# Banded attention stage: the rotary half-swap transfers are put out behind a pair's second transpose, and weight loads are asked for twelve units sooner

## The chip, the cores and the metric

The kernel runs on one core of one Trainium2 chip. The metric is the device time of one execution in microseconds; the time of a kernel is the median of its runs. Three runs of the kernel before took 1186.71, 1188.02 and 1188.46 us, so its time is 1188.02 us. Durations and waits in this text come from one further execution, taken under the hardware profiler: it took 1186.6 us, and its span from the first to the last instruction was 1184.9 us.

The engines are PE (matrix products; PEld is its weight load), DVE (vector), ACT (scalar functions), POOL (GpSimd) and SP, which here does nothing but issue DMA transfers. Each engine takes its instructions strictly in the order in which they stand in the program and waits in place where an input is missing.

## The reference

One decoder layer on 2048 tokens of width 1024. A normalised, modulated input `h` is multiplied by one wide matrix, and the product is cut into the inputs of two attentions. The second, the banded one, is what the change touches: queries and keys are rotated by position, each block of 128 queries sees its own and the preceding block of keys, and a learned sink joins the softmax.

```python
proj = h @ w_in[l]
qa, ka, va, fa, za, qb, kb, vb, zb = jnp.split(proj, split_points, axis=-1)
oa = forgetting_attention(qa, ka, va, fa + b_fgate[l])      # causal, 8 heads
oa = oa * jax.nn.silu(za)
qb = rope(qb, positions); kb = rope(kb, positions)
ob = sliding_window_sink_attention(qb, kb, vb, sinks[l])    # window 128, 8 query heads, 2 kv heads
ob = ob * jax.nn.silu(zb)
y = jnp.concatenate([oa, ob], axis=-1) @ w_out[l]
x = x + gate[:, None, :] * rms_norm(y, g_post[l])

def rope(x, positions):            # x1, x2: the two halves of a head's 64 columns
    return concatenate([x1 * cos - x2 * sin, x2 * cos + x1 * sin])
```

## The kernel before

Every matrix operand is split into a high and a low fp16 part, and a product is made of three fp16 products. The input projection is cut into **groups** of eight **units** (`proj_units`, L328; `value_units`, L346): one group makes 512 tokens of 128 output columns in one PSUM bank, of which there are three. The groups stand in one list, `punits`, and `fill` issues them unit by unit. A **key** such as `qb2`, `zb3` or `va1` names 128 columns of the weight matrix. What its weights need before their first unit hangs on `events`, at a lead counted in units: the load (`w_load`, 46 units ahead), the largest absolute value (`w_max`, L223, 36), the exchange of that value (`w_back`, 26), the scale, the high part (`w_high`, L266, on ACT) and the two halves of the low part (`w_low`, L272, on DVE). The raw weights have two buffers.

Work that follows a group, its evacuation, is put off by `after(n, f)`: `f` is issued at the n-th following `tick`.

**The banded stage** (about 160 to 414 us of the profile) runs 32 windows, `Pair(j, i)`: two query blocks of two heads each. It walks through the windows with four ticks to a window, and fills about 8.5 units of the projection between the ticks. In step n the program issues, in this order: the maxima of window n on DVE (L865), after the second tick the output products of window n-2 on PE (`pv`, L914), after the third tick the four exponentials of window n on ACT (L876), one tick later the rounding of its probabilities to fp16 on ACT (L893) with a DMA transpose of that high part (L894), one tick later, at the first tick of step n+1, the subtraction that leaves the low part on DVE (L898) with a second DMA transpose (L899), and at the end of step n the score products of window n+1 on PE (L851). The fp32 scores of a window have one buffer, so the maxima of window n+1 cannot start before the low part of window n is done. `pv` of a window needs both of its transposes.

**The rotation of a query group** is done in `evac_rope`. One tick after the group ACT copies the product to `qf` (L716), and SP issues four transfers of 32 partitions each that swap the halves into `qs` (L718). One tick later DVE multiplies the product by the cosine into `qc` (L721). In the banded stage (`turn_lag` 1) POOL multiplies `qs` by the sine at tick 6 (L731), DVE adds the two at tick 7 (L732), ACT rounds the sum to the high part of `stb` at tick 8 (L733), and DVE makes the low part at tick 9 (L725). `qf` and `qs` have one buffer each. The scores of the windows of that query group read `stb`.

**Weight loads in this stage** are not issued where they are asked for. `w_load` puts them on the list `queued`, and `load_now` empties it on SP right behind the second transpose of a window (or when the largest value is needed and the load is still on the list). Loads asked for before the stage are issued by POOL at once. The four swap transfers, in contrast, go to SP at the copy's tick, wherever that falls between the transposes.

After the stage come the causal attention (455 to about 1000 us) and the output projection. The change does not touch their instructions.

Of the kernel before, what the change touches and what calls it, by code (L numbers as in the profile page):

```python
# [14 lines left out]
AF = mybir.ActivationFunctionType  # L15
ALU = mybir.AluOpType
# [24 lines left out]
def hybrid_layer(  # L41
# [17 lines left out]
    V, A, G, PE, SP = nc.vector, nc.scalar, nc.gpsimd, nc.tensor, nc.sync  # L59
# [74 lines left out]
    sinT = swc.tile([P, S], F32, name="sinT")  # L134
# [26 lines left out]
    def kappa(pw, name):  # L161
        kap = const.tile([P, 1], F32, name=f"kap_{name}")
        V.tensor_scalar(kap[:], pw[:], pH[:], 0.125, op0=ALU.mult, op1=ALU.mult)
        return kap
# [22 lines left out]
    def after(n, f):  # L187
        late.append([n, f])
# [9 lines left out]
    kaps_seen = []  # L198
    first = ("kb", "vb", "zb0", "zb1")

    queued, banded = [], [False]

    def load_now():
        todo, queued[:] = queued[:], []
        for key, pieces in todo:
            w_load(key, pieces, SP)

    def w_load(key, pieces, eng=None):
        if banded[0] and eng is None:
            queued.append((key, pieces))  # L210
            return
        width = VB if key == "vb" else P
        raw = (vbw if key == "vb" else wpool).tile([P, KT, width], F32, tag="wraw", name=f"wr_{key}")
        o = 0
        for col0, n in pieces:
            (eng or G).dma_start(raw[:, :, o:o + n], w_in0[:, col0:col0 + n].rearrange("(k p) n -> p k n", p=P))
            o += n
        wq[key] = [raw]

    def w_max(key):  # L220
        if any(h[0] == key for h in queued):
            load_now()
        V.tensor_reduce(wmx[:, 0:1], wq[key][0][:], axis=AX.XY, op=ALU.max, apply_absolute_value=True)  # L223
        md, mt = mx_d[len(kaps_seen) % 3], wmt[len(kaps_seen) % 2]
        V.transpose(mt[:], wmx[:])
        kaps_seen.append(key)

        def put():
            G.dma_start(md[:].rearrange("(b j) o -> b (j o)", b=4),
                    mt[:].rearrange("(b r) j -> b r j", b=4)[:, 0, :])  # L230
            wq[key].append(md)

        if lag[0]:
            after(lag[0], put)
        else:
            put()

    def w_back(key):
        mxr = mxp.tile([P, P], F32, tag="mxr", name="mxr")
        G.dma_start(mxr[:], wq[key].pop().rearrange("p o -> (p o)").partition_broadcast(P))  # L240
        wq[key].append(mxr)

    def w_scale(key):

        floor = key[:2] == "qk"
        raw, mxr = wq[key]
        if key in first:
            mx2 = mxr
        else:
            mx2 = sm(1, "w_mx2")  # L250
            V.tensor_reduce(mx2[:], mxr[:], axis=AX.X, op=ALU.max)
        pw = sm(1, "w_pw")
        pow2_floor(pw[:], mx2[:], "w_p2")
        if floor:
            V.tensor_tensor(pw[:], pw[:], pfl[:], op=ALU.max)
        sw = sm(1, "w_sw")
        V.reciprocal(sw[:], pw[:])
        V.tensor_scalar(sw[:], sw[:], 2.0 ** 14, None, op0=ALU.mult)
        wq[key] = [raw, pw, sw]

    def w_high(key):
        raw, pw, sw = wq[key]
        width = VB if key == "vb" else P
        pool = vbw if key == "vb" else wpq if key[0] in "qk" else wpool
        whl = pool.tile([P, 2, KT, width], F16, tag="whl", name=f"wh_{key}")
        A.activation(whl[:, 0], raw[:], AF.Identity, scale=sw[:])  # L266
        wq[key].append(whl)

    def w_low(key, part, parts=2):
        raw, pw, sw, whl = wq[key]  # L270
        ks = slice(KT * part // parts, KT * (part + 1) // parts)
        V.scalar_tensor_tensor(whl[:, 1, ks], raw[:, ks], sw[:], whl[:, 0, ks], op0=ALU.mult, op1=ALU.subtract)  # L272
        if part == parts - 1:
            wq[key] = whl
            pws[key] = pw
# [9 lines left out]
    def col(name):  # L285
        return const.tile([P, 1], F32, name=name)

    def w_done(key):

        kind, j = key[:2], key[2:]  # L290
        pw = pws[key]
        if kind == "qk":
            kap = kappa(pw, key)
            scl[key] = col(f"scl_{key}")
            V.tensor_scalar(scl[key][:], kap[:], kap[:], 0.125, op0=ALU.mult, op1=ALU.mult)
            isc[key] = col(f"isc_{key}")
            V.reciprocal(isc[key][:], scl[key][:])
        elif kind == "qb":
            kap = kappa(pw, key)
            scl[key] = col(f"scl_{key}")  # L300
            V.tensor_scalar(scl[key][:], kap[:], kaps["kb"][:], 0.125, op0=ALU.mult, op1=ALU.mult)
        elif kind == "va":
            kaps[key] = kappa(pw, key)
        else:
            czs[key] = col(f"cz_{key}")
            V.tensor_scalar(czs[key][:], pw[:], pH[:], 2.0 ** -29, op0=ALU.mult, op1=ALU.mult)
            n = int(j) + (4 if kind == "zb" else 0)
            V.tensor_tensor(fac8[:, n:n + 1], kaps["vb" if kind == "zb" else f"va{j}"][:], czs[key][:], op=ALU.mult)

    def pieces(key):  # L310
        kind, j = key[:2], int(key[2:] or 0)
        if kind == "vb":
            return [(OFF_VB, P), (OFF_FA, 8)]
        if kind == "qk":
            return [(OFF_QA + j * 64, 64), (OFF_KA + j * 64, 64)]
        return [({"qb": OFF_QB, "kb": OFF_KB, "va": OFF_VA, "za": OFF_ZA, "zb": OFF_ZB}[kind] + j * P, P)]
# [133 lines left out]
    with tc.manual_schedule():  # L450
# [89 lines left out]
        rest, parts = TWO_PI, []  # L540
# [163 lines left out]
    turn_lag = [0]  # L704

    def evac_rope(ci, finish, pool):
        cols_ = slice(ci * CH, (ci + 1) * CH)

        def evac(ps, free):
            qf = swt.tile([P, CH], F32, tag="qf", name="qf")  # L710
            qs = swt.tile([P, CH], F32, tag="qs", name="qs")
            qc = op_.tile([P, CH], F32, tag="tz", name="qc")
            stg = (pool or abp).tile([P, 2, CH], F16, tag="st", name="stb")

            def copy():
                A.activation(qf[:], ps, AF.Copy, scale=PS_SCALE)  # L716
                for r in range(4):
                    SP.dma_start(qs[32 * r:32 * r + 32, :], qf[32 * (r ^ 1):32 * (r ^ 1) + 32, :])  # L718

            def cos():  # L720
                V.scalar_tensor_tensor(qc[:], ps, PS_SCALE, cosT[:, cols_], op0=ALU.mult, op1=ALU.mult)  # L721
                free()

            def low():
                V.tensor_tensor(stg[:, 1, :], qc[:], stg[:, 0, :], op=ALU.subtract)  # L725
                finish(stg)

            after(1, copy)
            after(2, cos)
            d = turn_lag[0]  # L730
            after(5 + d, lambda: G.tensor_tensor(qs[:], qs[:], sinT[:, cols_], op=ALU.mult))  # L731
            after(6 + d, lambda: V.tensor_tensor(qc[:], qc[:], qs[:], op=ALU.add))  # L732
            after(7 + d, lambda: A.activation(stg[:, 0, :], qc[:], AF.Copy))  # L733
            after(8 + d, low)

        return evac

# [188 lines left out]

    pkeys, punits = [], []

    def add(key, us):
        if key not in pkeys and key not in ("kb", "vb"):
            at = len(punits) - (24 if key[:2] == "za" else 0)
            leads = (46, 36, 26, 15, 11, 8, 7, 5) if key[:2] in ("va", "zb") else (46, 36, 26, 14, 9, 6, 4, 3)
            fs = (lambda: w_load(key, pieces(key)), lambda: w_max(key), lambda: w_back(key), lambda: w_scale(key),
                  lambda: w_high(key), lambda: w_low(key, 0), lambda: w_low(key, 1), lambda: w_done(key))
            for n, f in enumerate(fs):
                if key == "zb0":
                    if n >= 3:
                        events.setdefault(n + 9, []).append(f)  # L940
                elif key == "zb1":
                    if n >= 3:
                        events.setdefault((18, 20, 22, 24, 25)[n - 3], []).append(f)
                else:
                    events.setdefault(max(at - leads[n], n), []).append(f)
        if key not in pkeys:
            pkeys.append(key)
        punits.extend(us)
# [3 lines left out]
    for kind, j in (("zb", 0), ("zb", 1), ("va", 0), ("zb", 2), ("zb", 3), ("va", 1), ("va", 2)):  # L952
        key = f"{kind}{j}"
# [55 lines left out]
    N_PRO = len(punits)  # L1009
# [74 lines left out]
    with swa_order:  # L1084
# [18 lines left out]
        for n, wd in enumerate(windows):  # L1103
            goal = base + (N_SWA - base) * (n + 1) // NW
            todo = goal - pos[0]
# [27 lines left out]
        tick()  # L1133
        banded[0] = False
        load_now()
    swa.close()
    swx.close()
# [382 lines left out]
    with tc.manual_schedule():  # L1520
# [28 lines left out]
        for s, stp_ in enumerate(steps):  # L1549
# [7 lines left out]
            todo = []  # L1557
# [97 lines left out]
```

## Time and profile before

| | |
|---|---|
| median of 3 runs | 1188.02 us (1186.71 to 1188.46) |
| profiled execution | 1186.6 us, span 1184.9 us |
| PE busy over the span | 1122.8 us, 95% |
| DVE, ACT, POOL busy | 919.1, 677.6, 165.9 us |
| PE idle from 155 to 414 us | 259.0 us of time, 244.85 us busy |

The last row adds five stretches of the table of windows (155 to 200, 200 to 250, 250 to 300, 300 to 350, 350 to 414 us; PE busy 43.54, 47.10, 47.21, 46.88 and 60.12 us).

How to read what follows. A row of the timeline has the start in us, the duration, the engine, the line, the operation with output and input, how many instructions are merged in it, and in brackets how long the engine sat idle before it and what ended that. Rows of SP show the time that the issue of a transfer took on its queue, not when the data landed. A row of the table of windows has the stretch, its length, PE's busy time and count, the clock that was granted to PE as a share of full speed, the busy share of the DMA engines and GB/s.

### The profile page before, as it was taken

Reading aid. Unit: us, or ns where it says so; the run is one execution under the profiler, and the core shown is the slowest. Engines: PE = TensorE matmul, PEld = TensorE weight load, DVE = VectorE, ACT = ScalarE, POOL = GpSimd, SP = SyncE. Lnnn points to the kernel's source line nnn. Section 1 sums busy time; section 2 is a strip of 40 time slices with the busy share of each in tenths; the row PEclk is TensorE's granted clock in tenths of the full one; section 3 lists DMA queues with packets and bytes.
Section 4 is the critical chain, followed back from the end, with each engine's and each line's share of the span. In section 5 each row is a group of like instructions: output and inputs, shape, how many; then the busy total and the mean of one; then the engine's idle time right before and its main releaser. Section 6 shows DMA issues by size and latency. Waiting matters only on the chain. (4 is left out here: it accounts for less than half of the span.)

```text
span 1184.9 us, 27012 instructions
## 1 busy us (share of the span) xinstructions
PE 1122.8 (95%) x10490; PEld 655.1 (55%) x10490; DVE 919.1 (78%) x2329; ACT 677.6 (57%) x1122; POOL 165.9 (14%) x302
## 2 busy tenths in 40 slices
PE   5899998999989999999999999999999979999996
PEld 1466556644459855555555555555555545555553
DVE  6776577888787657889888897888878897767665
ACT  4676445565456434666766666666766788333331
POOL 1001122233232201211111111011000100000000
PEclk9999999999999999999999999999999989999999
DMA  9645336587667722333323323133121154465652
GB/s 331 213 137 158 94 88 123 113 150 143 141 132 119 130 63 70 78 93 78 85 68 103 75 61 86 45 90 64 40 48 46 59 156 156 147 191 168 210 172 78
DMA packets 162452, 136.36 MB, mean 115 GB/s; under 512 B 95356, under 2 KB 139428, under 8 KB 162324
## 3 DMA queue, kind: packets, MB, share of 16 engines
q1 hardware_dynamic: 152532, 106.65, 35.8%
q0 software_dynamic: 9456, 27.72, 8.9%
q8 instruction: 82, 1.34, 0.5%
q14 instruction: 46, 0.38, 0.1%
q10 hardware_dynamic: 336, 0.26, 0.1%
HBM read 70.97 MB, written 25.18 MB: 81 GB/s over the span
## 5 line engine op out<-in xcount | busy, mean ns | idle before, releaser
L1312 ACT ACTIVATE p<-sta,lift,scl_qk 128x1024 f32<-128x1024 f32 (+2 forms) x160 | 171.7, 1073 | 99.2 <-PE sta L1308 90.7
L328 PE MATMUL bk<-hT,wh_qk 128*128 128x512 f16 x768 | 194.6, 378 | 0.0
L1458 PE MATMUL bk<-wohl,oz 128*128 128x512 f16 x768 | 172.4, 379 | 1.9 <-ACT wohl L1398 0.8
L1323 DVE TENSOR_TENSOR pha<-p,pha 128x1024 f16<-128x1024 f32 (+2 forms) x160 | 169.3, 1058 | 0.2 <-ACT pha L1320 0.2
L1320 ACT ACTIVATE pha<-p 128x1024 f16<-128x1024 f32 (+2 forms) x160 | 148.1, 926 | 35.0 <-POOL p L1316 29.6
L1261 DVE TENSOR_REDUCE a_m<-bk 128x1 f32<-128x512 f32 x192 | 129.8, 684 | 43.6 <-PE bk L1258 43.1
L1458 PEld LDWEIGHTS <-oz 128*128 128x128 f16 x768 | 74.4, 99 | 83.9 <-issue 1.8
L1307 PE MATMUL sta<-T 128*128 128x512 f16 (+1 forms) x320 | 110.7, 351 | 10.5 <-ACT p L1312 10.5
L1333 PE MATMUL poa<-vt,pha 128*128 128x65 f16 x1088 | 117.6, 194 | 2.3 <-DVE ona L1342 2.3
L1336 PE MATMUL poa<-vt,pha 128*128 128x65 f16 x1088 | 117.2, 193 | 1.4 <-DVE pha L1323 1.4
L1335 PE MATMUL poa<-vt,pha 128*128 128x64 f16 x1088 | 117.5, 195 | 0.0
L328 PEld LDWEIGHTS <-wh_qk 128*128 128x128 f16 x768 | 72.4, 97 | 74.7 <-issue 0.6
L1333 PEld LDWEIGHTS <-pha 128*128 128x128 f16 x1088 | 102.4, 97 | 16.8 <-DVE ona L1342 3.2
L1258 PE MATMUL bk<-T 66*128 66x512 f16 (+2 forms) x320 | 109.9, 350 | 1.0 <-DVE a_m L1261 1.0
L1308 PE MATMUL sta<-T 69*128 69x512 f16 (+1 forms) x320 | 109.3, 352 | 0.0
L1335 PEld LDWEIGHTS <-pha 128*128 128x128 f16 x1088 | 101.7, 98 | 13.6 <-issue 0.3
L1336 PEld LDWEIGHTS <-pha 128*128 128x128 f16 x1088 | 101.5, 99 | 1.6 <-DVE pha L1323 1.6
L328 PE MATMUL bk<-hT,wh_za 128*128 128x512 f16 x384 | 99.8, 378 | 0.0
L346 PE MATMUL bk<-wh_va,hT 128*128 128x128 f16 x1536 | 94.3, 221 | 1.7 <-DVE wh_va L272 1.7
L328 PE MATMUL bk<-hT,wh_zb 128*128 128x512 f16 x384 | 92.7, 384 | 2.2 <-DVE wh_zb L272 2.2
L346 PEld LDWEIGHTS <-hT 128*128 128x128 f16 x1536 | 89.0, 99 | 8.3 <-issue 5.9
L1316 POOL TENSOR_SCALAR_AFFINE_SELECT p<-p 128x256 f32<-128x256 f32 x64 | 33.0, 515 | 420.6 <-ACT p L1312 417.9
(487 smaller groups left out, 1860.5 us busy)
## 6 DMA issues: line engine op xcount, KB each, us to landing
wa<-in_w_ada_dram SPq DMA_DIRECT2D x16, 512.0 KB
z_d<-tz POOLq DMA_DIRECT2D x32, 256.0 KB, 3.0
T<-stq SPq DMA_DIRECT2D x128, 64.0 KB
T<-o_d SPq DMA_DIRECT2D x16, 512.0 KB
T<-z_d SPq DMA_DIRECT2D x16, 512.0 KB
xr<-in_x_dram SPq DMA_DIRECT2D x16, 512.0 KB
out_dram<-yg SPq DMA_DIRECT2D x15, 512.0 KB
xt<-in_x_dram SPq DMA_DIRECT2D x12, 512.0 KB
```

Source lines behind the costliest of these rows:

```text
L328: PE.matmul(ps, whl[:, a, k, :], hT[ci][:, b, k, :], start=(k == 0 and n == 0), stop=(k == KT - 1 and n == 2))
L346: PE.matmul(ps[:, u * P:(u + 1) * P], hT[ci][:, a, k, u * P:(u + 1) * P], whl[:, b, k, :], start=(k == 0 and n == 0), stop=(k == KT - 1 an ...
L1258: PE.matmul(mx[:, :w], T[0:XM, 0, i * P:(i + 1) * P], T[0:XM, 2, pc * CH:pc * CH + w], start=True, stop=True)
L1261: V.tensor_reduce(m3[:, u, pc:pc + 1], mx[:, :w], axis=AX.X, op=ALU.max)
L1307: PE.matmul(self.st[:, o:o + w], T[:, 3, kb_], T[:, 1, qc], start=True, stop=False)
L1312: A.activation(self.p32[:, :self.w], self.st[:, :self.w], AF.Exp, scale=scl[f"qk{self.hd}"][:], bias=lift[:])
L1320: A.activation(self.ph[:, 0, :self.w], self.p32[:, :self.w], AF.Copy)
L1323: V.tensor_tensor(self.ph[:, 1, :self.w], self.p32[:, :self.w], self.ph[:, 0, :self.w], op=ALU.subtract)
L1333: PE.matmul(po[:, u, :], ph[:, 0, pq], vt[:, b, hd, 0:65], start=(self.first and n == 0 and u == 0), stop=False)
L1335: PE.matmul(po[:, u, 0:64], ph[:, 0, pq], vt[:, b, hd, 65:VW], start=False, stop=False)
L1336: PE.matmul(po[:, u, :], ph[:, 1, pq], vt[:, b, hd, 0:65], start=False, stop=(self.last and n == len(self.blocks) - 1))
L1458: PE.matmul(py, self.hl[:, i, k, :], w_slot(8 * j + k)[:, cc], start=(k == 0 and m_ == 0), stop=(k == KT - 1 and m_ == 2))
```

## The change

In the banded stage the copy no longer issues the swap. It puts it, with the four later steps of the rotation, on a list `swaps`; `load_now` empties that list ahead of the weight loads, so the swap goes out behind a window's second transpose, and the sine multiply, the add, the high part and the low part follow 4, 5, 6 and 7 ticks after that. Outside the stage everything is as before. And the loads of all keys that are asked for from the stage's first units on, `qk0` and the `qb`, `zb` and `va` keys, have a lead of 58 units in place of 46.

```diff
     def load_now():
+        todo, swaps[:] = swaps[:], []
+        for f in todo:
+            f()
         todo, queued[:] = queued[:], []
         for key, pieces in todo:
             w_load(key, pieces, SP)
...
             def copy():
                 A.activation(qf[:], ps, AF.Copy, scale=PS_SCALE)
+                if banded[0]:
+                    swaps.append(lambda: (swap(), rest(4)))
+                else:
+                    swap()
+                    rest(4 + turn_lag[0])
+
+            def swap():
                 for r in range(4):
                     SP.dma_start(qs[32 * r:32 * r + 32, :], qf[32 * (r ^ 1):32 * (r ^ 1) + 32, :])
+
+            def rest(d):
+                after(d, lambda: G.tensor_tensor(qs[:], qs[:], sinT[:, cols_], op=ALU.mult))
+                after(d + 1, lambda: V.tensor_tensor(qc[:], qc[:], qs[:], op=ALU.add))
+                after(d + 2, lambda: A.activation(stg[:, 0, :], qc[:], AF.Copy))
+                after(d + 3, low)
...
             after(1, copy)
             after(2, cos)
-            d = turn_lag[0]
-            after(5 + d, lambda: G.tensor_tensor(qs[:], qs[:], sinT[:, cols_], op=ALU.mult))
-            after(6 + d, lambda: V.tensor_tensor(qc[:], qc[:], qs[:], op=ALU.add))
-            after(7 + d, lambda: A.activation(stg[:, 0, :], qc[:], AF.Copy))
-            after(8 + d, low)
...
-    pkeys, punits = [], []
+    pkeys, punits, N_PRO = [], [], 10 ** 6
...
+            if at > N_PRO and (key == "qk0" or key[:2] not in ("qk", "za")):
+                leads = (58,) + leads[1:]
```

The order on PE is the same, instruction for instruction. On SP, here the issues from the first transpose of window 4 to the second of window 7, before (`ptb` is what a transpose writes, `sp` the rounded probabilities, `qs` and `qf` the swap, `wr` raw weights):

```order
L894 DMA_TRANSPOSE ptb<-sp_1938 128x8x128
L718 DMA qs<-qf 32x512 x4
L899 DMA_TRANSPOSE ptb<-sp_1936 128x8x128
L894 DMA_TRANSPOSE ptb<-sp_1937 128x8x128
L899 DMA_TRANSPOSE ptb<-sp_1938 128x8x128
L216 DMA wr_qb_2733<-in_w_in_dram 128x8x128
L894 DMA_TRANSPOSE ptb<-sp_1936 128x8x128
L718 DMA qs<-qf 32x512 x4
L899 DMA_TRANSPOSE ptb<-sp_1937 128x8x128
L894 DMA_TRANSPOSE ptb<-sp_1938 128x8x128
L899 DMA_TRANSPOSE ptb<-sp_1936 128x8x128
```

and the same windows with the change:

```order
L905 DMA_TRANSPOSE ptb<-sp_1938 128x8x128
L910 DMA_TRANSPOSE ptb<-sp_1936 128x8x128
L728 DMA qs<-qf 32x512 x4
L219 DMA wr_qb_2580<-in_w_in_dram 128x8x128
L905 DMA_TRANSPOSE ptb<-sp_1937 128x8x128
L910 DMA_TRANSPOSE ptb<-sp_1938 128x8x128
L905 DMA_TRANSPOSE ptb<-sp_1936 128x8x128
L910 DMA_TRANSPOSE ptb<-sp_1937 128x8x128
L728 DMA qs<-qf 32x512 x4
L905 DMA_TRANSPOSE ptb<-sp_1938 128x8x128
L910 DMA_TRANSPOSE ptb<-sp_1936 128x8x128
```

No swap stands between the two transposes of a window any more (before, this was so in windows 4, 6, 14, 21 and 23), and the load of `qb2` stands one window sooner. The other loads that SP issues in the stage move by one window too, `zb2` and `va1` by two.

On DVE, from the low part of window 9 to that of window 10 (the rows of the maxima, L865 or L876, are thinned to the last), before:

```order
L732 TENSOR_TENSOR qc<-qc,qs 128x512
L898 TENSOR_TENSOR sp_1937<-sm__3131,sp_1936 128x1024
...
L868 TENSOR_SCALAR b_nb<-b_m 128x2
L725 TENSOR_TENSOR stb<-qc,stb 128x512
L920 TENSOR_TENSOR on<-pob,b_ri 128x256
L272 SCALAR_TENSOR_TENSOR wh_qb_3255<-wr_qb_2733,w_sw,wh_qb_3255 128x512
L721 SCALAR_TENSOR_TENSOR qc<-bk_135,cosT 128x512
L272 SCALAR_TENSOR_TENSOR wh_qb_3255<-wr_qb_2733,w_sw,wh_qb_3255 128x512
L898 TENSOR_TENSOR sp_1936<-sm__3237,sp_1938 128x1024
```

and with the change:

```order
L909 TENSOR_TENSOR sp_1937<-sm__3131,sp_1936 128x1024
...
L879 TENSOR_SCALAR b_nb<-b_m 128x2
L732 TENSOR_TENSOR qc<-qc,qs 128x512
L931 TENSOR_TENSOR on<-pob,b_ri 128x256
L275 SCALAR_TENSOR_TENSOR wh_qb_3256<-wr_qb_2580,w_sw,wh_qb_3256 128x512
L741 TENSOR_TENSOR stb<-qc,stb 128x512
L737 SCALAR_TENSOR_TENSOR qc<-bk_135,cosT 128x512
L275 SCALAR_TENSOR_TENSOR wh_qb_3256<-wr_qb_2580,w_sw,wh_qb_3256 128x512
L909 TENSOR_TENSOR sp_1936<-sm__3238,sp_1938 128x1024
```

The add L732 stood ahead of window 9's low part and of window 10's maxima; now it stands behind these maxima. On ACT, windows 12 and 13, before (L733 rounds the rotated queries, L876 are the exponentials, L893 the rounding of the probabilities):

```order
L733 ACTIVATE stb<-qc 128x512
L716 ACTIVATE qf<-bk_136 128x512
L876 ACTIVATE sm__3441,b_rs<-sm__3441,b_nb 128x257 x4
L893 ACTIVATE sp_1936<-sm__3441 128x1024
L378 ACTIVATE tz<-bk_135,cz_zb_3000 128x512
L876 ACTIVATE sm__3541,b_rs<-sm__3541,b_nb 128x257 x4
L893 ACTIVATE sp_1938<-sm__3541 128x1024
L733 ACTIVATE stb<-qc 128x512
```

and with the change:

```order
L719 ACTIVATE qf<-bk_136 128x512
L733 ACTIVATE stb<-qc 128x512
L887 ACTIVATE sm__3440,b_rs<-sm__3440,b_nb 128x257 x4
L904 ACTIVATE sp_1936<-sm__3440 128x1024
L381 ACTIVATE tz<-bk_135,cz_zb_3000 128x512
L887 ACTIVATE sm__3543,b_rs<-sm__3543,b_nb 128x257 x4
L904 ACTIVATE sp_1938<-sm__3543 128x1024
L719 ACTIVATE qf<-bk_137 128x512
```

The high part L733 stands just ahead of the exponentials of a window in both, but the add that it reads has moved behind the maxima of that same window. It stands so, add behind the maxima and high part ahead of the exponentials, in windows 6, 8, 23 and 25 before, and with the change in all fourteen windows that have one: 3, 5, 6, 8, 10, 12, 14, 16, 18, 20, 22, 23, 25 and 27.

More of the change, by code (lines that the diff above doesn't have):

```diff
@@ L199, in hybrid_layer @@
     first = ("kb", "vb", "zb0", "zb1")
-    queued, banded = [], [False]
+    queued, swaps, banded = [], [], [False]
     def load_now():
+        todo, swaps[:] = swaps[:], []
+        for f in todo:
+            f()
         todo, queued[:] = queued[:], []
```

## The prediction

> **What bounds the kernel now.** I read the page's head first, then PE's timeline through the banded stage, then the table of windows for its clock.
>
> ```profile
> span 1184.9 us, 27012 instructions
> PE 1122.8 (95%) x10490; PEld 655.1 (55%) x10490; DVE 919.1 (78%) x2329; ACT 677.6 (57%) x1122; POOL 165.9 (14%) x302
> ```
>
> PE is busy for 95% of the span and its order of work does not change, so the change can only win what PE loses in this stage. PE's timeline shows each loss as an idle time in brackets, with what ended it:
>
> ```profile
> 165.12 5.41 PE L346 MATMUL bk<-wh_va,hT 128*128 128x128 f16 x94 [1.24 <-DVE wh_va L272]
> ...
> 206.48 0.82 PE L914 MATMUL pob<-vb,ptb 128*128 128x64 f16 x22 [2.90 <-DMA ptb<-sp]
> ...
> 257.84 0.86 PE L914 MATMUL pob<-vb,ptb 128*128 128x64 f16 x24 [0.58 <-DVE on L920]
> ...
> 279.48 3.83 PE L328 MATMUL bk<-hT,wh_zb 128*128 128x512 f16 x10 [2.21 <-DVE wh_zb L272]
> ...
> 312.29 0.86 PE L914 MATMUL pob<-vb,ptb 128*128 128x64 f16 x24 [0.86 <-DVE on L920]
> ...
> 334.77 0.81 PE L914 MATMUL pob<-vb,ptb 128*128 128x64 f16 x22 [1.37 <-DMA ptb<-sp]
> ...
> 351.95 0.81 PE L914 MATMUL pob<-vb,ptb 128*128 128x64 f16 x22 [2.85 <-DMA ptb<-sp]
> ...
> 380.78 0.86 PE L914 MATMUL pob<-vb,ptb 128*128 128x64 f16 x24
> ...
> 396.63 0.86 PE L914 MATMUL pob<-vb,ptb 128*128 128x64 f16 x24 [1.16 <-DVE on L920]
> ...
> 401.39 3.40 PE L346 MATMUL bk<-wh_va,hT 128*128 128x128 f16 x58 [0.44 <-DVE wh_va L272]
> ```
>
> These nine gaps sum to 13.61 us: 7.12 wait for a transpose (`ptb`), 3.89 for weights (`wh`), 2.60 for `on`, the division of an output that leaves its PSUM tile free. The table of windows shows what follows three of the longest (columns: stretch, length, PE busy, granted clock, DMA share, GB/s):
>
> ```profile
> 208.00:212.00 4.00, 4.00 (x47) 0.64 0.71 174
> 279.50:283.50 4.00, 4.00 (x22) 0.62 0.34 88
> 352.00:356.00 4.00, 4.00 (x82) 1.00 0.47 85
> ```
>
> After the gaps of 2.90 and 2.21 us PE ran 4 us at a clock of 0.64 and 0.62, which loses 4 x 0.36 + 4 x 0.38 = 2.96 us; after the one of 2.85 us it lost nothing. So the **ceiling** is 13.61 + 2.96 = 16.6 us: 1186.6 - 16.6 = 1170.0 us for the profiled execution. The Trainium skill ("TensorE: Matmul & The Clock Gate", section "Part 1: The HAM clock gate") says that the clock is lowered after an idle window of about 3.4 us, and that these windows run free of the kernel. By that no gap of this stage would be long enough and the ceiling would be 13.6 us; the first two rows speak against it, so I keep the 2.96.
>
> **Part 1, the swap leaves the place between two transposes.** SP's queue, in two of the places (start, time of issue):
>
> ```profile
> 198.63 2.85 SPq L718 DMA_DIRECT2D qs<-qf  x4
> 201.57 1.25 SPq L899 DMA_TRANSPOSE ptb<-sp  x1
> ...
> 345.73 2.42 SPq L718 DMA_DIRECT2D qs<-qf  x4
> 348.25 1.25 SPq L899 DMA_TRANSPOSE ptb<-sp  x1
> ```
>
> The four issues hold SP for 2.85 and 2.42 us, and the second transpose follows at once, 4.91 and 3.70 us ahead of the output product that waits for it (206.48, 351.95). Put out behind it, they let it go by about that much sooner, if its low part was ready. That covers the gaps at 206.48 and 351.95 and the like one at 334.77, 7.12 us with 1.44 of clock. No instruction is added: 14 swaps of four issues stay, behind the transposes.
>
> **Part 2, loads one to two windows sooner.** The largest value of the weights (L223) waits on DVE until its load lands. Idle time before that line, by transfer (us, count), and its longest early case:
>
> ```profile
>   DMA wr_qb<-in_w_in_dram: 5.9, 2
>   DMA wr_zb<-in_w_in_dram: 5.1, 2
>   DMA wr_va<-in_w_in_dram: 4.3, 2
> ...
> 158.05 1.22 DVE L223 TENSOR_REDUCE wmx<-wr_qb 128x1 f32<-128x1024 f32 x1 [4.46 <-DMA wr_qb<-in_w_in_dram]
> ```
>
> No single wait there is above 4.46 us, and a window takes about 7 to 8 us (the 194.83 below, over 25), so a load that stands one window sooner ends all of them. The raw weights' buffer is released by the low part of earlier weights, which DVE has done by then, so SP should not stand at the load. DVE waits in place: what it waits there delays the next low part, and with it the transposes, `wh` and `on`. Of the waits, 4.46 us lie before window 2; the other 5.9 - 4.46 = 1.4 of `qb`, 5.1 of `zb` and 4.3 of `va`, together 10.8 us, lie between the low parts of windows 2 and 27.
>
> **Part 3, the add moves behind the maxima.** This is the price, and nothing in the words of the change names it. A window is a loop: low part, maxima, exponentials, rounding, low part. DVE's timeline shows the loop in a window with only the low part of a rotation, in one with the add and the high part ahead of the rounding, and in one with the high part ahead of the exponentials:
>
> ```profile
> 172.02 1.23 DVE L898 TENSOR_TENSOR sp<-sm__2043,sp 128x1024 f16<-128x1024 f32 x1 [1.70 <-ACT sp L893]
> ...
> 179.91 1.22 DVE L898 TENSOR_TENSOR sp<-sm__2180,sp 128x1024 f16<-128x1024 f32 x1 [0.26 <-ACT sp L893]
> ...
> 252.56 1.22 DVE L898 TENSOR_TENSOR sp<-sm__3337,sp 128x1024 f16<-128x1024 f32 x1
> ...
> 256.17 0.68 DVE L725 TENSOR_TENSOR stb<-qc,stb 128x512 f16<-128x512 f32 x1
> ...
> 258.57 1.23 DVE L898 TENSOR_TENSOR sp<-sm__3441,sp 128x1024 f16<-128x1024 f32 x1 [0.79 <-ACT sp L893]
> ...
> 334.12 1.55 DVE L898 TENSOR_TENSOR sp<-sm__4492,sp 128x1024 f16<-128x1024 f32 x1 [0.65 <-ACT sp L893]
> ...
> 338.63 0.69 DVE L732 TENSOR_TENSOR qc<-qc,qs 128x512 f32<-128x512 f32 x1
> 339.36 0.63 ACT L733 ACTIVATE stb<-qc 128x512 f16<-128x512 f32 x1 [4.69 <-DVE qc L732]
> ...
> 343.08 1.23 DVE L898 TENSOR_TENSOR sp<-sm__4591,sp 128x1024 f16<-128x1024 f32 x1 [2.37 <-ACT sp L893]
> ...
> 374.74 1.20 DVE L898 TENSOR_TENSOR sp<-sm__5187,sp 128x1024 f16<-128x1024 f32 x1
> ```
>
> The plain loop is 258.57 - 252.56 = 6.01 us. In the last kind ACT stands idle for 4.69 us until the add, rounds for 0.63, and only then begins the exponentials, which otherwise start while DVE is still at the second half of the maxima. That window takes 343.08 - 334.12 = 8.96 us; I take 0.78 off as an estimate of other work in it, so 8.96 - 0.78 - 6.01 = 2.17 us is the price. Four windows have this order before and fourteen with the change: ten more cost 10 x 2.17 = **21.7 us** of the loop.
>
> Against it stands what the ten windows lose that hold the rotation now. The row at 258.57 bounds it below: with the low part L725 inside, the loop is still the plain 6.01, so taking it out gives 0. The row at 179.91 bounds it above: 7.89 - 6.01 = 1.88 us with add, high part and low part in one loop. Of the ten, by the order, five are of that kind (windows 2, 4, 17, 19, 21) and five have add and low part in two loops (9 to 16 and 26). I take 1.88 for the first and 0.3 for the second, an estimate near the lower row: 5 x 1.88 + 5 x 0.3 = **10.9 us**.
>
> **The sum.** The low parts of windows 2 and 27 lie 374.74 - 179.91 = 194.83 us apart. With the change: -10.8 (loads) - 10.9 + 21.7 = 0. Parts 2 and 3 cancel over the 25 windows, and what is left is that the stage begins sooner. The wait of 4.46 goes; I count 3.5 us of it, an estimate, as window 0 also needs its scores. So the low part of window 27 starts at about 371.2. Its output product needs 1.20 for the low part and the time from the second transpose's issue to PE, 4.91 and 3.70 in the rows of part 1; at 4.0 that is 5.2, or 376.4, against 380.78 with no wait there now: -4.4 us. Behind it the gaps of 1.16 and 0.44 should go with `qk0`'s sooner load: -1.6. Together -6.0 us: 1180.6 us for the profiled execution. The median of the runs shown is 1188.0, which is 1.4 above that execution, so the **forecast is 1182.0 us**. Its own range, with the relief between 7 and 15 us, is 1178 to 1185.6. PE will then wait less at the old places and somewhat in new ones, mostly for `ptb`, as DVE's loop becomes what sets the stage.
>
> **The rivals.**
>
> *Full recovery, 1171.4 us.* PE is never late: the loop has slack where I count none, because the new order's idle time on DVE takes in weights, cosine and `on`, which today stand ahead of a low part. That gives the ceiling, 1170.0 + 1.4. For it speaks that the windows behind 8.96 us ones have low parts that follow in 6 to 8 us; against it that 14 such windows in 25, with the rest at 6 to 7, need some 7.8 us each, no less than now.
>
> *No change, about 1188 us.* The relief is 4.9 us in place of 10.9 (about 0.5 a window). What the loads give back, the loop takes; the gaps change their names from swaps and weights to `ptb`.
>
> *Slower, 1194.7 us.* The sine multiply on POOL falls on DVE. The rows that carry it:
>
> ```profile
> 322.42 1.44 DVE L868 TENSOR_SCALAR b_nb<-b_m 128x2 f32<-128x2 f32 x1
> 322.56 1.26 POOL L731 TENSOR_TENSOR qs<-qs,sinT 128x512 f32<-128x512 f32 x1
> ...
> 324.81 0.17 DVE L868 TENSOR_SCALAR b_nb<-b_m 128x2 f32<-128x2 f32 x1
> ```
>
> An instruction of 0.17 us took 1.44 beside the multiply: 1.27 us of the loop, between the maxima and the exponentials. Now swap and multiply follow the second transpose by a fixed number of ticks, so the multiply meets the same part of the loop in every rotation: either always or never. If in the ten moved windows it is this part, they cost 12.7 us more: -6.0 + 12.7 = +6.7. It decides from 0.6 us a window on. The Trainium skill ("SBUF — State Buffer", section "SBUF: two separate sides") says that DVE and GpSimd share a port pair as an exclusive lock, held for the whole instruction, so that the loser waits. The trace agrees: the stretch of 1.27 is the multiply's 1.26. Against it: POOL has the swap after it lands, some 4 us behind the issue, which may as well meet the exponentials.
>
> *The queries come too late, about 1184 us.* The scores of windows 4 and 6 read rotated rows that are now finished up to a window later. If PE waits there, up to the 2.9 us it waits at 206.48 today, part 1's first gap only moves: 1182.0 + 2 or so. It stays within the forecast's range.
>
> *It doesn't do what it says:* loads held in SP's queue behind waiting transposes would land no sooner. The order shows them a full window ahead, so I give this little, inside "no change".
>
> **How the numbers follow.** A measurement of this kernel can tell about 0.2%, 2.4 us, from no change. Forecast with the late queries 0.49, full recovery or near it (below 1178) 0.13, no change 0.17, slower 0.21. That makes faster 0.62, same 0.17, slower 0.21. The range leaves out the last of the full recovery and the top of the slower case: 1172.5 to 1193 us; the faster cases alone span 1172.5 to 1185.6.
>
> **What would show it.** Right for part 1: no idle time of PE at 206, 335 and 352 us that ends with a transpose behind a swap. For part 2: DVE's waits for `wr` gone, and window 0's maxima about 3.5 us sooner. For part 3: ACT idle ahead of the high part in fourteen windows, loops of about 9 us there and 6 to 7 elsewhere, and the low part of window 27 near 371 us. The slower case would show as b_nb rows of over a microsecond in most rotated windows. I am wrong if loops with the high part ahead of the exponentials take under 8 us, or if PE's new waits for `ptb` in the stage pass 10 us in sum.

## The result, and the profile after

The kernel with the change takes 1181.24 us (median of 4 runs, 1178.54 to 1183.09), the one before 1187.66 us in the same comparison (4 runs, 1186.71 to 1188.46): a ratio of 0.9944, with a 95% interval of 0.9932 to 0.9956. The forecast was 1182.0 us. The profiled execution has a span of 1179.3 us, 5.6 us less than before.

PE's waits in the stage, first before and then after, are in the view that groups waits (engine, output and line of the waiting instruction, what it waited for; sum in us, times, longest; 155 to 410 us):

```profile
PE pob L914 <- DMA ptb<-sp: 7.1, 3, 2.9
PE pob L914 <- DVE on L920: 2.8, 4, 1.2
PE bk L328 <- DVE wh_zb L272: 2.2, 1, 2.2
PE bk L346 <- DVE wh_va L272: 1.7, 2, 1.2
```

```profile
PE pob L925 <- DMA ptb<-sp: 6.6, 6, 2.6
PE pob L925 <- DVE on L931: 1.2, 2, 1.0
```

The waits for weights are gone and those for `on` more than halved, but the waits for a transpose are nearly as long in sum as they were. They are in other places. PE's timeline after has the longest of them, the start of the output product of window 27 (377.04), and the first row behind the stage:

```profile
223.96 0.81 PE L925 MATMUL pob<-vb,ptb 128*128 128x64 f16 x22 [0.92 <-DMA ptb<-sp]
...
262.78 0.81 PE L925 MATMUL pob<-vb,ptb 128*128 128x64 f16 x22 [2.62 <-DMA ptb<-sp]
...
338.10 1.00 PE L925 MATMUL pob<-vb,ptb 128*128 128x64 f16 x22 [1.58 <-DMA ptb<-sp]
...
370.16 0.82 PE L925 MATMUL pob<-vb,ptb 128*128 128x64 f16 x22 [0.92 <-DMA ptb<-sp]
...
377.04 0.86 PE L925 MATMUL pob<-vb,ptb 128*128 128x64 f16 x24
...
409.07 0.30 PE L1220 MATMUL bk<-identh,cst 128*69 128x128 f16 x2 [1.06 <-DVE vt L358]
```

The wait at 370.16 shows a price of the hold. SP's queue ahead of it:

```profile
358.08 3.31 SPq L728 DMA_DIRECT2D qs<-qf  x4
361.43 0.59 SPq L219 DMA_DIRECT2D wr_va<-in_w_in_dram  x1
362.46 1.37 SPq L905 DMA_TRANSPOSE ptb<-sp  x1
363.95 1.91 SPq L910 DMA_TRANSPOSE ptb<-sp  x1
```

The rounding that the first transpose needs was done at 361.33 us and the low part that the second needs at 362.59, so swap and load ahead of them held them for 1.1 and 1.4 us. Put behind one window's second transpose, a swap stands ahead of the next window's first. The row at 377.04 has no idle time: PE comes late to it from the wait at 370.16, and does not wait there for that window's own transposes.

The same row behind the stage (409.07) starts at 414.74 us before. So the stage ends 5.67 us sooner, and from there to the end of the span both executions need 770.2 us: the whole gain lies in this stage.

The clock table after (stretch, length, PE busy, granted clock, DMA share, GB/s) shows what two of the new gaps cost on top:

```profile
262.80:266.80 4.00, 4.00 (x31) 0.58 1.08 205
338.10:342.10 4.00, 4.00 (x30) 0.57 0.38 77
```

That is 4 x 0.42 + 4 x 0.43 = 3.4 us, where the prediction counted 2.96 before. The difference comes from where the stretches of before were cut: over the 10 us from 206 and from 278 us the granted clock before is 0.83, as it is with the change over the 10 us from 262 and from 337 us. Each of the four costs 1.7 us, so the clock takes 3.4 us in both kernels. DVE's timeline after shows the maximum that waited 4.46 us before, now without a wait, the low parts of windows 2 and 27, and one loop of the kind that the change makes ten more of (the high part on ACT, L733, is put in by its start):

```profile
154.84 1.21 DVE L226 TENSOR_REDUCE wmx<-wr_qb 128x1 f32<-128x1024 f32 x1
...
175.70 1.23 DVE L909 TENSOR_TENSOR sp<-sm__2182,sp 128x1024 f16<-128x1024 f32 x1 [0.37 <-ACT sp L904]
...
305.25 1.23 DVE L909 TENSOR_TENSOR sp<-sm__4174,sp 128x1024 f16<-128x1024 f32 x1
...
307.70 1.28 DVE L879 TENSOR_SCALAR b_nb<-b_m 128x2 f32<-128x2 f32 x1
...
310.15 0.69 DVE L732 TENSOR_TENSOR qc<-qc,qs 128x512 f32<-128x512 f32 x1
310.87 0.63 ACT L733 ACTIVATE stb<-qc 128x512 f16<-128x512 f32 x1 [2.64 <-DVE qc L732]
...
314.59 1.23 DVE L909 TENSOR_TENSOR sp<-sm__4276,sp 128x1024 f16<-128x1024 f32 x1 [2.23 <-ACT sp L904]
...
370.49 1.18 DVE L909 TENSOR_TENSOR sp<-sm__5186,sp 128x1024 f16<-128x1024 f32 x1
```

From the low part of window 2 to that of window 27 the change needs 370.49 - 175.70 = 194.79 us; before it was 194.83. The loop is as slow as it was, and it starts 4.2 us sooner.

### The profile page after: what moved, and what is told of

Same layout as the page of the kernel before. It is cut to its first block, busy times and chain, and to the rows that moved or that the text cites. A ratio compares the mean times of both kernels' runs of the same rounds, so it can differ in the third digit from the quotient of the medians.

```text
span 1179.3 us, 26982 instructions
## 1 busy us (share of the span) xinstructions
PE 1123.0 (95%) x10490; PEld 653.9 (55%) x10490; DVE 916.8 (78%) x2329; ACT 677.5 (57%) x1122; POOL 167.4 (14%) x302
## 5 line engine op out<-in xcount | busy, mean ns | idle before, releaser
L1348 PEld LDWEIGHTS <-pha 128*128 128x128 f16 x1088 | 101.7, 98 | 13.6 <-issue 0.3
```

The lines of the kernel that those rows point to most:

```text
L1348: PE.matmul(po[:, u, 0:64], ph[:, 0, pq], vt[:, b, hd, 65:VW], start=False, stop=False)
```

## The experiments

Three theories stood. Mine: the sooner loads win time, and the add's new place behind the maxima takes nearly as much back. Rival A: the gain is the swap's leaving the place between the two transposes. Rival B: the loop of low part, maxima, exponentials and rounding is not what sets the stage.

**The swap hold alone.**

```diff
-                leads = (58,) + leads[1:]
+                leads = (46,) + leads[1:]
```

> The swap hold alone, loads at 46 units as before. Theory (loads and the add's new place cancel): the load waits of 10.8 us between windows 2 and 27 and the 4.46 us before window 0 stay, and the ten more windows with the high part ahead of the exponentials still cost 21.7 less 10.9 us, so the low part of window 27 starts near 385 us and the kernel is slower than before, about 1195 us (1191 to 1199). Rival A (the gain is the swap's leaving the place between two transposes): 1180 to 1184 us, the gaps at 206, 335 and 352 us gone. Rival B (the add's place costs nothing): within 2 us of before.

Measured: 1204.04 us, ratio 1.0133 (1.0116 to 1.0150). Rival A falls: the transposes are free of swaps in this kernel, and it is 16.8 us slower than before. It is also 9 us slower than I expected. The idle time before the maximum of new weights says why (transfer, us, count):

```profile
  DMA wr_zb<-in_w_in_dram: 10.6, 2
  DMA wr_va<-in_w_in_dram: 6.4, 2
  DMA wr_qb<-in_w_in_dram: 5.3, 2
  DMA wr_qk<-in_w_in_dram: 5.1, 2
```

In sum 27.4 us, against 19.3 before. SP's queue in this kernel, and the wait on DVE that belongs to it:

```profile
189.65 1.34 SPq L910 DMA_TRANSPOSE ptb<-sp  x1
191.16 2.42 SPq L728 DMA_DIRECT2D qs<-qf  x4
193.68 0.52 SPq L219 DMA_DIRECT2D wr_zb<-in_w_in_dram  x1
```

```profile
197.83 1.22 DVE L226 TENSOR_REDUCE wmx<-wr_zb 128x1 f32<-128x1024 f32 x1 [5.05 <-DMA wr_zb<-in_w_in_dram]
```

The held swap goes ahead of the load on the same queue, so the load is issued 2.5 us later than it could be.

**The loads alone.** The swap is issued at the copy's tick, as before:

```diff
-                if banded[0]:
-                    swaps.append(lambda: (swap(), rest(4)))
-                else:
-                    swap()
-                    rest(4 + turn_lag[0])
+                swap()
+                rest(4 + turn_lag[0])
```

> Loads at 58 units, the swap issued at the copy's tick as before. Theory: DVE's waits for loads go and nothing is paid for the add, so the low part of window 27 starts 10 us or more sooner than before and PE is hardly late: 1172 to 1177 us, faster than the change. Rival A (the swap between transposes is what counts): the waits for ptb of 7.1 us and 1.4 us of clock stay, about 1180 to 1183 us, no faster than the change.

Measured: 1173.6 us (1173.08 to 1174.64), ratio 0.9883 (0.9868 to 0.9898). Faster than the change by 7.6 us. No maximum waits for a load any more. Swaps still stand between the two transposes of windows 4, 6, 21 and 23, the same four as in the trace of before (the one counted there for window 14 was issued by 271.65 us, ahead of that window's first transpose at 271.81). Even so PE's waits for transposes shrink, and only the one of 1.9 us is for a window (23) with a swap between them:

```profile
PE pob L922 <- DMA ptb<-sp: 3.2, 2, 1.9
...
PE bk L331 <- DVE wh_qb L275: 0.3, 1, 0.3
```

So the hold, as it is written, costs 7.6 us on top of the sooner loads (7.2 by the ratios).

**The rotation later, in two steps.** If the hold costs time through the add behind the maxima and the high part ahead of the exponentials, then moving both on should win it back. Eleven of the fourteen rotations have slack for that; the first two and the eleventh keep their ticks. One tick later the add stands during the exponentials and the high part between them and the rounding; two ticks later the high part stands behind the rounding.

```diff
-    turn_lag = [0]
+    turn_lag, n_rot = [0], [0]
...
                 if banded[0]:
-                    swaps.append(lambda: (swap(), rest(4)))
+                    n_rot[0] += 1
+                    d = 4 if n_rot[0] in (1, 2, 11) else 6
+                    swaps.append(lambda: (swap(), rest(d)))
```

The second kernel has 5 in place of 6.

> The change, with sine multiply, add, high part and low part of eleven of the fourteen rotations two ticks later (6, 7, 8 and 9), so that the add stands during the exponentials and the high part behind the rounding. Theory: the eleven loops of about 9 us fall to between 6 and 7 us, the low part of window 27 starts at 358 us or as soon as PE lets it, PE's waits for ptb in the stage nearly go, 1171 to 1175 us. Rival B (the loop of low part, maxima, exponentials and rounding does not set the stage): the time stays at 1180 to 1182 us.

> As the run before, one tick later in place of two (5, 6, 7 and 8): the add during the exponentials, the high part between the exponentials and the rounding. Theory: each of the eleven loops still holds 0.6 us of the high part on ACT, so loops of 7 to 8 us, 1173 to 1178 us. Rival B: 1180 to 1182 us.

Measured: 1169.85 us, ratio 0.9846 (0.9831 to 0.9861), with two ticks; 1167.88 us (1167.24 to 1168.92), ratio 0.9835 (0.9820 to 0.9849), with one. Rival B falls: a change in nothing but the place of four small operations (the sine multiply on POOL, the add, the high part and the low part) in eleven loops is worth 13.4 us against the change. Fewer meetings of the multiply with DVE are not the reason: in windows 3 to 27 the b_nb rows (the small operation on DVE between a window's maxima and its exponentials) are longer than their usual 0.17 us by 6.8 us in sum with one tick, by 5.1 us in the change. Both times lie below what was expected. Both kernels beat the one before, the change and the loads alone. With one tick, ACT hardly waits for the add any more: of the eleven rotations two wait longer than 0.25 us (0.54 and 1.35 us). The loop that took 9.34 us in the change, the one that gains most, takes 303.95 - 297.32 = 6.63 us; the eleven together take 85.1 us, 96.8 in the change.

```profile
297.32 1.23 DVE L911 TENSOR_TENSOR sp<-sm__4174,sp 128x1024 f16<-128x1024 f32 x1
...
302.34 0.63 ACT L735 ACTIVATE stb<-qc 128x512 f16<-128x512 f32 x1
...
303.95 1.23 DVE L911 TENSOR_TENSOR sp<-sm__4275,sp 128x1024 f16<-128x1024 f32 x1 [0.25 <-ACT sp L906]
```

The idle time of ACT ahead of the high part over the whole kernel (us, times) tells the same in one row each: before, the change, the change one tick later.

```profile
  DVE qc L732: 47.3, 15
```

```profile
  DVE qc L732: 61.5, 18
```

```profile
  DVE qc L734: 21.0, 9
```

In the kernel with one tick PE's table has no idle time for 195 us from 155 on: it runs at PE's own pace, as the four stretches show.

```profile
155.00:200.00 45.00, 45.00 (x558) 1.00 0.57 110
200.00:250.00 50.00, 50.00 (x501) 1.00 0.76 145
250.00:300.00 50.00, 50.00 (x430) 1.00 0.84 155
300.00:350.00 50.00, 50.00 (x663) 1.00 0.70 136
```

I had expected two ticks to be the better one. They differ by 2.0 us, with intervals that overlap. In the two profiled executions the stage ends 0.92 us apart (396.21 and 397.13), of which PE's one wait with two ticks is 0.43; the larger part lies behind the stage (769.3 and 771.6 us to the end), where the two issue the same. So it is not shown that one tick is better than two.

**The swap ahead of the second transpose.** `swap_now` empties the list `swaps`; all other engines keep the change's order:

```diff
             def low():
                 for p, (hi, lo) in cuts:
                     V.tensor_tensor(lo, p, hi, op=ALU.subtract)
+                swap_now()
                 SP.dma_start_transpose(self.ptt[:, 1, 0:self.nt, :], part[1][:, 0:n])
                 load_now()
```

> The change, with the held swaps put out just ahead of the second transpose instead of behind it; order of all other engines as in the change. Theory: the swap only needs the copy, so SP issues it while DVE still makes the low part, and the transpose goes at most 1.3 us later in fourteen windows, which only those windows feel in which PE waits for ptb: 1181 to 1185 us. Rival A (the place on SP between the transposes is what the change wins): back to 1186 us or more.

Measured: 1182.55 us (1181.36 to 1185.08), ratio 0.9966 (0.9953 to 0.9978). Beside the change's 0.9944 in another comparison, the place behind the transpose is worth some 1.3 us by the medians and 2.6 by the ratios, with intervals that just overlap. This is a net figure. With the swap ahead, the sine multiply meets the b_nb rows less often (in windows 3 to 27 they are 2.0 us too long in sum, 5.1 in the change), while PE's waits for a transpose grow from 6.6 to 9.1 us; so the place by itself may be worth up to some 3 us more, an estimate from these sums. Rival A's 1186 us or more did not come, and the loads alone, with four swaps between transposes, are faster than the change.

**The loads ahead of the held swaps**, at 46 units:

```diff
     def load_now():
-        todo, swaps[:] = swaps[:], []
-        for f in todo:
-            f()
         todo, queued[:] = queued[:], []
         for key, pieces in todo:
             w_load(key, pieces, SP)
+        todo, swaps[:] = swaps[:], []
+        for f in todo:
+            f()
```

> The swap hold with loads at 46 units, as in the run of the swap hold alone, but with the loads issued ahead of the held swaps. That run made DVE's waits for loads longer than before (27.4 against 19.3 us). Theory: each load then stood behind four swap issues, 2.4 us; put ahead of them the waits return to about 19 us and the time falls from 1204 to 1194 to 1199 us. Rival: the loads are late because the loops are longer, and the time stays at 1202 to 1205 us.

Measured: 1195.59 us, ratio 1.0069 (1.0055 to 1.0082): 8.4 us less than with the swaps ahead (7.6 by the ratios). The waits sum to 19.6 us, as before the change, and the wait shown above falls from 5.05 to 3.06 us:

```profile
194.22 1.22 DVE L226 TENSOR_REDUCE wmx<-wr_zb 128x1 f32<-128x1024 f32 x1 [3.06 <-DMA wr_zb<-in_w_in_dram]
```

The theory holds: half of the 16.8 us that the swap hold alone loses is its place ahead of the loads on SP.

**The rotation one tick later, with loads at 46 units.**

> The kernel with eleven rotations one tick later, with loads at 46 units in place of 58. Theory: waits for loads add up with the loop of the softmax; the loops of the swap hold alone add up to 247 us, eleven of them get about 2 us shorter, and PE alone needs 213 us, so PE is late by about 10 us: 1177 to 1183 us. Rival C (with the short loops there is slack for the waits, the loads do not matter any more): up to 1172 us.

Measured: 1189.61 us (1187.37 to 1190.31), ratio 1.0016 (1.0005 to 1.0026). The direction is right and rival C falls, but the size was off: the twelve units are worth 21.7 us here, where I had expected 10 to 15. The waits for loads sum to 26.9 us, nearly those of the swap hold alone, and one of them alone takes 6.06 us:

```profile
314.05 1.22 DVE L226 TENSOR_REDUCE wmx<-wr_va 128x1 f32<-128x1024 f32 x1 [6.06 <-DMA wr_va<-in_w_in_dram]
```

I had also credited each of eleven loops with 2 us; with the load waits taken out, ten of them are shorter by 0.6 to 2.0 than in the swap hold alone and one is longer by 0.2, a fall of about 1.2 in the mean. The 0.63 us of the high part stay on ACT between the exponentials and the rounding; how much of the miss that is was not followed.

## Why the prediction was right, step by step

The mechanism and the sum held; two of its terms were too small by about 3 us each, in opposite directions. For the change they come from the differences of neighbouring low parts in the two traces, window by window, with the load waits taken out. Of the ten new windows, window 20 is the one quoted above: 9.34 us, 6.02 before (313.55 to 319.57). Of the relieved ones, window 17 takes 6.04 us (283.73 to 289.77), 8.49 before (286.96 to 295.45). The ends are these rows, of before and of after:

```profile
286.96 1.21 DVE L898 TENSOR_TENSOR sp<-sm__3870,sp 128x256 f16<-128x256 f32 x2
295.45 1.23 DVE L898 TENSOR_TENSOR sp<-sm__3964,sp 128x1024 f16<-128x1024 f32 x1 [0.25 <-ACT sp L893]
...
313.55 1.23 DVE L898 TENSOR_TENSOR sp<-sm__4174,sp 128x1024 f16<-128x1024 f32 x1 [0.26 <-ACT sp L893]
319.57 1.23 DVE L898 TENSOR_TENSOR sp<-sm__4283,sp 128x1024 f16<-128x1024 f32 x1 [1.39 <-ACT sp L893]
```

```profile
283.73 1.21 DVE L909 TENSOR_TENSOR sp<-sm__3864,sp 128x256 f16<-128x256 f32 x2 [1.23 <-ACT sp L904]
289.77 1.22 DVE L909 TENSOR_TENSOR sp<-sm__3966,sp 128x1024 f16<-128x1024 f32 x1 [0.41 <-ACT sp L904]
```

| term, us | forecast | measured |
|---|---|---|
| waits for loads, windows 2 to 27 | -10.8 | -10.8 |
| ten windows with the high part ahead of the exponentials | +21.7 | +25.2 |
| windows that lose the rotation | -10.9 | -13.8 |
| the other windows | 0 | -0.7 |
| low part of window 2 sooner | -3.5 | -4.2 |
| all of these: low part of window 27 | -3.5 | -4.3 |
| output product of window 27, with all of these in it | -4.4 | -3.7 |
| behind it, to the stage's end | -1.6 | -1.9 |
| sum of the last two | -6.0 | -5.7 |

The forecast's relief of 10.9 us has two slips. It counts window 2, which ends where the 25 windows begin; the 13.8 measured are of the nine others, and window 2's own 1.0 us is in the -4.2. And 1.88 us was no upper bound: windows 4, 17, 19 and 21 lose 2.38, 2.45, 2.37 and 1.65 us, and windows 9, 11, 13, 15 and 26 lose 0.8 to 1.2 each where 0.3 was taken. The output product of window 27 starts 6.55 us after the low part, in place of 5.2, because PE itself was late.

Both large errors are about the size of what the b_nb rows show, which last 0.17 us but longer where they meet the sine multiply. In the nine windows that lose the rotation they were 4.1 us too long in sum and are no longer; in the ten that get it they were not too long and are now, by 3.7 us. Over windows 3 to 27 that makes 5.1 us in both kernels. The forecast took its price from window 23, where the two do not meet, and its relief from window 2, where the row is only 0.3 us too long, so the terms had little of this cost. No run moves the multiply alone, so this is read from the traces and not shown by an experiment.

- **Part 1** (swap away from between the transposes) was right in that the three old gaps went, and the sum gave it no term of its own; the swap put ahead of the transpose again puts a net 1.3 to 2.6 us on it. The sign given for it held only for the old places: at 370.16 PE waits again for a transpose behind a swap. The hold has a cost that I had only as a rival at the edge, "loads held in SP's queue": four swap issues stand ahead of each load. In the change the twelve units hide it, since no load is waited for in these windows; without them it costs 8 us.
- **Part 2** was right: of 19.3 us of waits, 1.1 us are left (for a later `qk` key, behind the stage). In the change it is worth more than the forecast said, 22.8 us by the difference of the medians (1204.04 to 1181.24), because it also covers those 8. Window 0's maxima start 2.7 us sooner (159.44 to 156.74), not 3.5, as there they wait for the scores; its low part starts 3.2 us sooner.
- **Part 3** was right in kind: the loops with the high part ahead of the exponentials last 7.5 to 10.0 us, 8.9 in the mean, as the "8.96" had it on the whole, not in each. My limit of being wrong, loops under 8 us, is touched by windows 8 and 16 (7.89 and 7.54); the other limit is not, as PE's waits for `ptb` sum to 6.6 us. Window 20 shows the price itself: 9.34 - 6.02 = 3.3 us where 2.17 was forecast, and 1.28 - 0.17 = 1.1 us of it is the b_nb row there, of the kind that the slower rival named. Without that it is 2.2.
- **The slower rival** was right in its mechanism and wrong in its frequency. The long b_nb rows (0.85, 0.84, 1.28 and 1.17 us) stand in 4 of 14 rotations, as many as before, not in most. What failed is its "either always or never": of the ten moved windows six have a b_nb row that is 0.3 to 1.1 us too long, and four have none. Their 3.7 us are as much as the 3.5 by which the ten windows cost more than forecast.
- **Full recovery** was not reached by the change, and is exceeded by the kernel one tick later: 1167.9 against 1171.4 us. That is 2.7 us more than the 16.6 of my ceiling, by the medians of that comparison (1187.19 - 1167.88 = 19.3). The ceiling left out an idle time of 0.22 us (195.93) and 0.45 us of clock outside the two 4 us stretches. Another 0.8 us lies behind the stage (770.2 us before, 769.3 with one tick), which neither kernel changes; the last 1.2 us stay open.
- **The median** was 0.8 us from the forecast. The two errors of 3 us cancelled, and the forecast did not know why, so that this closeness is partly luck; the signs and the order of the terms are not, as the runs with one part alone show: +16.8 us for the hold and -13.6 us for the loads. Both together are -6.4 and not the +3.2 of their sum, as the sooner loads take away the 8 us that the hold costs them on SP. One slip is in the range: with a relief of 7 us it ends at 1185.9, not 1185.6.

## What to carry to other kernels

A transfer that is put later on a queue takes its consumers with it: follow each of them to the place in the in-order engines where it now lands, above all between the work that starts a serial loop and the loop's next stage. Here the add, the high part and the low part, 0.6 to 0.7 us each, came later with the swap that was held, and cost more than the stall that the hold ended: with the loads put first on SP the hold alone is still 8.0 us slower than before (1195.59 against 1187.57). And where a change joins a hold to a sooner issue, measure each half alone: one of them may be paying for the other.

## What the runs showed of the hardware

The clock after a gap does not follow from the gap's length alone. These stretches of 4 us follow gaps of 2.56 us (the rotation one tick later, loads at 46) and 6.03 us (the swap hold alone):

```profile
259.40:263.40 4.00, 4.00 (x41) 1.00 0.69 71
```

```profile
266.80:270.80 4.00, 4.00 (x31) 0.50 0.13 38
```

The first kept full clock, while 2.62 us in the change cost 42% of the clock for 4 us and 2.21 us before cost 38%. In the traces the clock falls in steps: it is 0.50 for 3.41 us, or twice that, and 1.00 otherwise. Here is the kernel before with its gaps of 2.90 and 2.85 us, in stretches of 3.41 us counted from such a step:

```profile
204.06:207.47 3.41, 0.99 (x24) 1.00 1.01 175
207.47:210.88 3.41, 3.41 (x30) 0.50 0.88 196
...
347.42:350.83 3.41, 1.68 (x10) 1.00 0.66 134
350.83:354.24 3.41, 2.29 (x52) 1.00 0.79 162
```

The next step before begins at 279.15 us, 71.68 us on, which is 21 stretches of 3.41 us. Ahead of the two steps PE was busy for 0.99 and 1.54 us of the stretch, ahead of the two in the change for 0.79 and 0.87. The gap of 2.85 us is shared by two stretches with 1.68 and 2.29 us of work, and the clock stays. So what counts here is how little PE works between two edges of a fixed grid. The limit is not sharp: with the loads first, 1.63 us (199.97 to 203.39) cost clock and 1.44 us (356.99 to 360.40) did not. The Trainium skill ("TensorE: Matmul & The Clock Gate", section "Part 1: The HAM clock gate") has the clock lowered after an idle window of about 3.4 us that runs free of the kernel. The free-running window and its length agree with these rows. That it has to be idle from end to end does not: gaps of 2.21, 2.62 and 2.90 us are shorter and cost clock, with up to 1.54 us of work in the stretch.
